# Low halves of the MLP's weights made by an accumulating DMA instead of a subtraction on VectorE

## The chip, the cores and the metric

The kernel runs on one core of one Trainium2 chip. The core has a matrix engine (TensorE, PE in the profile; PEld are its weight loads), a vector engine (VectorE, DVE), a scalar engine (ScalarE, ACT), a general engine (GpSimd, POOL) and a queue engine (SyncE, SP), each with its own program, and 16 DMA engines that move data between HBM and the on-chip SBUF. Matmul results go to PSUM. The metric is the device time of one execution in microseconds (us), the median of several runs.

## The reference

One layer of a streaming encoder on x of [1, 512, 1024] in float32: three token mixers side by side, their gated sum and an output projection, a cross-attention into 256 memory tokens, and then the gated MLP that this case is about:

```
def conv_ffn(h, w_up, conv_w, conv_b, w_down):
    u = causal_dwconv(h @ w_up, conv_w) + conv_b
    a, b = jnp.split(u, 2, axis=-1)
    return (jax.nn.silu(a) * b) @ w_down
...
        x = x + conv_ffn(rmsnorm(x, norm_ffn[l]), w_up[l], ffn_conv[l], ffn_conv_b[l], w_down[l])
```

`w_up` is [1024, 5632] and `w_down` [2816, 1024], both float32; the convolution is causal, of width 3.

## The kernel before

All activations lie with channels on the 128 partitions and the 512 tokens along the row. The weights come as a stream of 168 units of [128, 1024] float32 (512 KB), eight blocks of [128, 128] each. TensorE multiplies in a rounded 32-bit format (fp32r in the profile). To keep float32 accuracy, each weight unit and each activation tile is cut in two: a high part, which is the value rounded to fp32r, and a low part, which is the value less the high part. A product then takes three matmuls for each block: high by high, high weights by low activations, low weights by high activations.

A unit is handled by three lines. `load_unit` (L139 to L146) has SP load it from HBM into a `wraw` buffer. `split_unit` (L148 to L156) has ACT write the rounded copy into a `whi` buffer (L154) and DVE write the difference of `wraw` and `whi` into a `wlo` buffer (L155). `WB = (3, 2, 2)` gives the number of buffers: three for `wraw`, two each for `whi` and `wlo`. A buffer is filled anew when its last reader is done. `mm3` (L171 to L178) issues a unit's matmuls: for each of its eight blocks the two with the high weights (L175, L176), and then the eight with the low weights (L178), a *low run* below. So a unit costs 24 matmuls, 16 with `whi` and 8 with `wlo`.

The MLP is the last part. Its up projection (L879 to L893) goes over 22 pairs of output tiles, one unit each: 44 units, through `project` (L183). The result `up` is scaled by `r_f` (L885, the norm's factor, on DVE), put through the convolution (`uc`: one step on ACT, L887, and two on DVE, L889), and after each second unit through silu on ACT (L891) and a product on DVE (L892), which is split again into `hid` tiles (L162 on ACT, L163 on DVE). The norm's factor `r_f` is worked out at the start of the MLP from a matmul `xfps` (L871) through three steps on ACT (`rfa`, `rfb`: L216 to L218) and three on DVE. The down projection (L895 to L908) goes over 8 output tiles `dn`, each over 22 blocks, so that a unit can end in the middle of a tile: 22 units, through `split_unit` (L902). Its results are added to the residual (L907) and stored by SP (L908).

The order of the instructions on each engine isn't that of the code. A scheduler places them by its own simulated timeline, with the data dependencies and the buffers as limits; each engine then runs its own list in order, and an instruction that waits holds up all that stand behind it on its engine. POOL has no instruction in the MLP, and issues no DMA anywhere.

Of the kernel before, what the change touches and what calls it, by code (L numbers as in the profile page):

```python
# [36 lines left out]

# [1 line left out]
COLS = {}  # L39
# [15 lines left out]

# [1 line left out]
UNITS = {}  # L57
# [9 lines left out]
def build(nc, tc, ctx, x_t, mem_t, w, cols_d, const_d, unit_d, out_t, dbg=None):  # L67
# [13 lines left out]

    work = tiles_of("work", "n", 4)        # short-lived
    awork = tiles_of("work", "w", 8)
# [29 lines left out]
    def in_one_go(after, tiles, func):  # L113
        """func on tiles in place, behind the instruction `after`, with one load of its table"""
        with tc.issue_after(after.ins), tc.high_priority():
            for t in tiles:
                S.activation(t, t, func)
            exp_ln_tables()
# [16 lines left out]

# [1 line left out]
    units = {}  # L137
# [10 lines left out]
    def split_unit(u):  # L148
        """a unit of the weight stream as an exact sum of two float32r operands"""
        raw = units.pop(u) if u in units else load_unit(u)  # L150
        hi = wp.tile([P, 1024], F32R, tag="whi", name=f"whi{u}", bufs=WB[1])
        lo = wp.tile([P, 1024], F32R, tag="wlo", name=f"wlo{u}", bufs=WB[2])
        for s in [slice(0, T), slice(T, 2 * T)] if u == 0 else [slice(0, 2 * T)]:
            S.activation(hi[:, s], raw[:, s], AF.Copy)  # L154
            V.tensor_tensor(lo[:, s], raw[:, s], hi[:, s].bitcast(F32), ALU.subtract)  # L155
        return hi, lo  # L156

    def split(src, alloc, name):
        """src as hi + lo"""
        hi = alloc(name + "h", F32R)  # L160
        lo = alloc(name + "l", F32R)
        S.activation(hi, src, AF.Copy)  # L162
        V.tensor_tensor(lo, src, hi.bitcast(F32), ALU.subtract)  # L163
        return hi, lo
# [6 lines left out]
    def mm3(ps, unit, blocks, xs, first, last):  # L171
        """ps += the blocks of a unit times xs, without the product of the low parts"""
        hi, lo = unit
        for i, (b, (xh, xl)) in enumerate(zip(blocks, xs)):
            PE.matmul(ps, hi[:, b], xh, start=first and i == 0, stop=False)  # L175
            PE.matmul(ps, hi[:, b], xl, start=False, stop=False)  # L176
        for i, (b, (xh, _)) in enumerate(zip(blocks, xs)):
            PE.matmul(ps, lo[:, b], xh, start=False, stop=last and i == len(xs) - 1)  # L178

    def block(i, n=P):  # L180
        return slice(i * P, i * P + n)

    def project(u, xs, name, n=T):  # L183
        ps = dense_ps(name)
        mm3(ps[:, :n], split_unit(u), [block(k) for k in range(KC)], xs, True, True)
        return ps
# [16 lines left out]
    def project_heads(u, ys, name, n=4):  # L203
        """[512, 1024] weights, two output tiles in a unit"""
        for g in range(n):
            unit = split_unit(u + g)
            for q in range(2):
                ps = dense_ps(f"{name}{2 * g + q}")
                mm3(ps, unit, [block(4 * q + k) for k in range(4)], ys, True, True)
                yield 2 * g + q, ps  # L210

    def rsqrt(ps, name, scale, n=T, work=work):
        """-2 / sqrt(ps * scale + eps), with a Newton step"""
        a = work(name + "a", F32, n)
        b = work(name + "b", F32, n)
        S.activation(a, ps, AF.Ln, bias=eps, scale=scale)  # L216
        S.activation(a, a, AF.Exp, scale=-0.5)
        S.activation(b, a, AF.Square, scale=math.sqrt(scale))  # L218
        V.scalar_tensor_tensor(b, ps, EPS / scale, b, ALU.add, ALU.mult)
        V.scalar_tensor_tensor(a, b, -3.0, a, ALU.add, ALU.mult)  # L220
        return a

    def head_norm(src, name, scale, n=T, work=work, psum=misc_ps, light=False):
        """-2 / sqrt(sum of src^2 * scale + eps) on every partition"""
        sq = work(name + "s", F32, n)
# [47 lines left out]

# [1 line left out]
    hs = []  # L275
# [14 lines left out]

# [1 line left out]
    xs, acc = [], None  # L292
# [10 lines left out]
    V.tensor_scalar(r_x, rsqrt(ps, "rx", 1.0 / D), -0.5, None, ALU.mult)  # L303
# [1 line left out]
    gl = cp.tile([P, H, 4], F32, tag="gl", name="gl")  # L305
# [36 lines left out]
    def convolve(g, base):  # L342
        """silu(conv(projection)) of the tiles of q, k or v"""
        conv[g] = cs = [ptile(f"{g}{h}") for h in range(H)]
# [6 lines left out]

# [1 line left out]
    R = 96  # L353
# [7 lines left out]
    def scalars():  # L361
# [24 lines left out]
        V.tensor_tensor(rl[:R], rows[:R], rh[:R].bitcast(F32), ALU.subtract)  # L386
        # token on partition: [.., token block, row]
        ps = misc_ps("rcol")
# [3 lines left out]
        V.tensor_scalar(ngc, rc[:, :, 2], -1.0, None, ALU.mult)  # L392
        # beta, beta * exp(gc), exp(g_last - gc)
        S.activation(beta, rc[:, :, 1], AF.Exp)
# [3 lines left out]
    def select(ps, kind, h, stop=True):  # L398
        """a row of the scalars on every partition"""
        sel = sp.tile([P, P], F32R, tag="sel", name=f"sel_{kind}{h}")  # L400
# [19 lines left out]
    def prep_head(h):  # L420
# [5 lines left out]
        q, k = cq, ck  # L426
        # the decay, [j, i] by chunks, 0 for j > i
        pt = gdn_ps(f"pt{h}")
# [11 lines left out]
        S.activation(tail[:, :, h], tail[:, :, h], AF.Exp)  # L440
        # A^T without its factors beta_i, and attn^T
        pk = gdn_ps(f"pk{h}")
# [13 lines left out]
        V.tensor_tensor(att, pq, et, ALU.mult)  # L456
        # token-major keys and values
        pkt = gdn_ps(f"pkt{h}")
# [11 lines left out]

    # the inverses of the 32 x 32 diagonal blocks of I + A by elimination, a block's
    # even or odd columns on a partition
    inverse = []
# [29 lines left out]
    def expand(dst, src, h):  # L503
        """the 32 x 32 blocks of a head on the diagonals of its chunks"""
        G.tensor_tensor(dst.rearrange("p (t m c) -> p t m c", t=4, m=4),
                        src[:, 4 * h:4 * h + 4, None, :].to_broadcast([P, 4, 4, 32]),
                        cst("blk")[:, None, :, None].to_broadcast([P, 4, 4, 32]), ALU.mult)
# [10 lines left out]
    def invert(h):  # L518
        """(I + A)^-T of the chunks from that of the blocks on their diagonals: with D these and
        M = A D^-1 without these blocks, M^4 = 0 and (I + A)^-1 = D^-1 (I - M + M^2 - M^3)"""  # L520
        xcomp, ycomp = inverse
# [46 lines left out]
    def qkv_head(u, h, name, norm, alloc):  # L568
        """q^T, k^T and [key, dv] by key blocks"""
        out = alloc(h)  # L570
# [19 lines left out]
    def packed(name, kinds):  # L590
        """[P, 128], .. [P, 512] of each kind, the halves of a kind's tile shared"""
        out, half = [], None
# [9 lines left out]

# [1 line left out]
    ya = []  # L604
# [40 lines left out]

# [1 line left out]
    mixed = []  # L647
# [20 lines left out]

# [1 line left out]
    tri_r = cp.tile([P, 2, P], F32R, tag="tri_r", name="tri_r")  # L670
# [42 lines left out]

# [1 line left out]
    sz, yb = [], []  # L715
# [62 lines left out]

# [1 line left out]
    xs_mem = split_mem(mem_sb, "mem", ztile)  # L780
# [7 lines left out]

# [1 line left out]
    acc = None  # L790
# [11 lines left out]

# [1 line left out]
    def memory_key(h):  # L804
# [69 lines left out]

# [1 line left out]
    cross.close()  # L876
    open_pool("hidden", ctx)
    hid = []
    for m in range(NF):  # L879
        ab = []  # L880
        for z in range(2):
            j = m + NF * z
            ps = project(UNITS["up"] + 2 * m + z, xf, f"up{j}")
            u = awork(f"u{j}")
# [11 lines left out]
    for m in range(KC):  # L896
        ps = dense_ps(f"dn{m}")
        k = 0
        while k < NF:
            c = m * NF + k  # L900
            if c % 8 == 0:
                unit = split_unit(UNITS["down"] + c // 8)  # L902
            n = min(8 - c % 8, NF - k)
# [23 lines left out]
def unit_columns():  # L927
    """[P, 32, 16]: the even (on even partitions) or odd columns of the unit matrix"""
    i = np.arange(P)
# [3 lines left out]
def layout(inputs):  # L933
# [3 lines left out]
    def tiles(a, n):  # L937
        """[K, M] -> [units, P, 1024] streaming (output tile, k chunk) blocks of [P, 128]"""
        k, m = a.shape
# [5 lines left out]
    def tokens(a):  # L945
        """[1024, 512] -> [4, P, 1024] streaming k chunks"""
        return a.reshape(4, 2, P, 512).transpose(0, 2, 1, 3).reshape(4, P, 1024)

    def by_head(a):
        """[q | k | v] weights as q, k, v of a head after the other"""  # L950
        return tiles(a, 12).reshape(3, H, P, 1024).transpose(1, 0, 2, 3).reshape(12, P, 1024)
# [75 lines left out]
```

## Time and profile before

| | us |
|---|---|
| median of 3 runs | 1073.2 |
| lowest and highest run | 1072.76 and 1074.09 |
| span of the profiled execution, first to last instruction | 1072.4 |

The page gives for the profiled execution's own time its span, 1072.4 us. In it, the MLP's first matmul starts at 699.54 us and its last low run at 1066.78, so that the MLP with its end takes about a third of the time. The page's 40 slices show the four compute engines and the DMA engines; each digit is the busy share of a slice of 26.8 us in tenths:

```profile
PE   6999999999999999999999998999999999999998
DVE  5987566886454443454577667667776667742221
ACT  6689677856263646574546557544444444431110
POOL 0000100101010000000000000000000000000000
PEclk9999999999999999999999999999999999999999
DMA  5232212121211122122244233122222222233330
```

The MLP is the last 14 of the 40. The queue table shows what the DMA engines carry (packets, MB, share of the 16 engines' span); q1 is SP's:

```profile
q1 hardware_dynamic: 27648, 95.26, 27.1%
HBM read 93.41 MB, written 2.10 MB: 89 GB/s over the span
```

### The profile page before, as it was taken

The numbers are of one execution on the slowest core, as the hardware profiler recorded it, in microseconds if no ns is written. First come the engines' busy times: TensorE is split into PE (matmuls) and PEld (weight loads), VectorE is DVE, ScalarE is ACT, GpSimd is POOL, SyncE is SP. The second block draws the span as 40 slices with busy tenths as digits, with TensorE's granted clock in tenths as the row PEclk, the third lists the DMA queues.
The fourth block names the chain that finished last, engine by engine and source line by source line (L and its number), as shares of the span: only waits on it lengthen the run. The fifth ranks groups of instructions, "written<-read, shape, count | busy, mean of one in ns | idle before, by whom it ended". The sixth has DMA issues, their size and how long they took to land.

```text
span 1072.4 us, 12705 instructions
## 1 busy us (share of the span) xinstructions
PE 1055.4 (98%) x4868; PEld 858.3 (80%) x4868; DVE 638.3 (60%) x1002; ACT 556.3 (52%) x894; POOL 31.6 (3%) x81
## 2 busy tenths in 40 slices
PE   6999999999999999999999998999999999999998
PEld 4887888778888888888888886778888888888886
DVE  5987566886454443454577667667776667742221
ACT  6689677856263646574546557544444444431110
POOL 0000100101010000000000000000000000000000
PEclk9999999999999999999999999999999999999999
DMA  5232212121211122122244233122222222233330
GB/s 209 79 98 98 79 61 77 61 88 59 80 59 60 59 64 74 60 65 97 94 147 168 90 107 99 41 97 99 90 90 95 98 99 92 91 103 108 118 117 20
DMA packets 27853, 96.33 MB, mean 90 GB/s; under 512 B 3088, under 2 KB 3344, under 8 KB 27536
## 3 DMA queue, kind: packets, MB, share of 16 engines
q1 hardware_dynamic: 27648, 95.26, 27.1%
q8 instruction: 38, 0.62, 0.2%
q10 hardware_dynamic: 144, 0.26, 0.1%
q14 instruction: 23, 0.19, 0.1%
HBM read 93.41 MB, written 2.10 MB: 89 GB/s over the span
## 4 chain that ended last, share of the span: by engine, by line
PE 96%; DVE 1%; ACT 1%; DMA 1%; issue 0%; SPq 0%; DVEq 0%; ACTq 0%
PE up L176 8%; PE up L178 8%; PE up L175 8%; PE g L176 4%; PE g L175 4%; PE g L178 4%; PE dn L178 4%; PE dn L176 4%; PE dn L175 4%; PE wo L176 1%; PE s L175 1%; PE f L178 1%; PE f L175 1%; PE s L176 1%; PE wo L178 1%; PE wo L175 1%
## 5 line engine op out<-in xcount | busy, mean ns | idle before, releaser
L154 ACT ACTIVATE whi<-wraw 128x1024 fp32r<-128x1024 f32 (+1 forms) x168 | 177.1, 1054 | 286.0 <-PE up L176 86.1
L155 DVE TENSOR_TENSOR wlo<-wraw,whi 128x1024 fp32r<-128x1024 f32 (+1 forms) x168 | 204.7, 1219 | 144.2 <-PE dn L178 49.2
L176 PE MATMUL up<-xfl,whi 128*128 128x512 f32 x352 | 139.3, 396 | 0.0
L175 PE MATMUL up<-xfh,whi 128*128 128x512 f32 x352 | 138.7, 394 | 0.0
L178 PE MATMUL up<-xfh,wlo 128*128 128x512 f32 x352 | 88.9, 395 | 0.0
L178 PEld LDWEIGHTS up<-xfh,wlo 128*128 128x128 f32 x352 | 66.3, 188 | 15.7 <-issue 0.2
L176 PEld LDWEIGHTS up<-xfl,whi 128*128 128x128 f32 x352 | 66.3, 188 | 15.7 <-issue 0.2
L175 PEld LDWEIGHTS up<-xfh,whi 128*128 128x128 f32 x352 | 66.3, 188 | 15.5
L175 PE MATMUL g<-hh,whi 128*128 128x512 f32 x192 | 76.9, 401 | 0.0
L176 PE MATMUL g<-hl,whi 128*128 128x512 f32 x192 | 76.8, 400 | 0.0
L889 DVE SCALAR_TENSOR_TENSOR uc<-u,cols,uc 128x511 f32<-128x511 f32 (+1 forms) x88 | 65.3, 747 | 1.4
L887 ACT ACTIVATE uc<-u,cols 128x512 f32<-128x512 f32 x44 | 35.8, 816 | 45.2 <-DVE u L885 45.0
L885 DVE TENSOR_TENSOR u<-up,r_f 128x512 f32<-128x512 f32 x44 | 30.2, 688 | 40.4 <-PE up L178 40.4
L178 PE MATMUL g<-hh,wlo 128*128 128x512 f32 x192 | 52.3, 402 | 0.0
L178 PEld LDWEIGHTS g<-hh,wlo 128*128 128x128 f32 x192 | 35.9, 188 | 8.3 <-issue 0.2
L176 PEld LDWEIGHTS g<-hl,whi 128*128 128x128 f32 x192 | 36.2, 188 | 7.8 <-issue 0.2
L175 PEld LDWEIGHTS g<-hh,whi 128*128 128x128 f32 x192 | 36.2, 188 | 7.7
L175 PE MATMUL f<-hh,whi 128*128 128x512 f32 x64 | 26.0, 406 | 0.0
L175 PE MATMUL s<-hh,whi 128*128 128x512 f32 x64 | 25.7, 402 | 0.0
L176 PE MATMUL s<-hl,whi 128*128 128x512 f32 x64 | 25.5, 398 | 0.0
L176 PE MATMUL wo<-msl,whi 128*128 128x512 f32 x64 | 25.3, 396 | 0.0
L176 PE MATMUL f<-hl,whi 128*128 128x512 f32 x64 | 25.3, 395 | 0.0
(968 smaller groups left out, 2288.1 us busy)
## 6 DMA issues: line engine op xcount, KB each, us to landing
wraw<-w SPq DMA_DIRECT2D x166, 512.0 KB, 3.3
x<-x_t SPq DMA_DIRECT2D x8, 256.0 KB, 7.2
xr<-x_t SPq DMA_DIRECT2D x2, 1024.0 KB, 6.2
out<-out SPq DMA_DIRECT2D x8, 256.0 KB, 2.0
mem_sb<-mem_t SPq DMA_DIRECT2D x4, 256.0 KB, 6.5
wraw<-w SPq DMA_DIRECT2D x2, 256.0 KB, 4.7
inv<-unit ACTq DMA_DIRECT2D x1, 256.0 KB, 3.9
const<-const SPq DMA_DIRECT2D x1, 194.0 KB, 6.4
```

The source lines that it names most:

```text
L154: S.activation(hi[:, s], raw[:, s], AF.Copy)
L155: V.tensor_tensor(lo[:, s], raw[:, s], hi[:, s].bitcast(F32), ALU.subtract)
L175: PE.matmul(ps, hi[:, b], xh, start=first and i == 0, stop=False)
L176: PE.matmul(ps, hi[:, b], xl, start=False, stop=False)
L178: PE.matmul(ps, lo[:, b], xh, start=False, stop=last and i == len(xs) - 1)
L885: V.tensor_tensor(u, ps, r_f, ALU.mult)
L887: S.activation(c, u, AF.Identity, bias=col("ffn_conv_b", j), scale=col("ffn_conv", 3 * j + 2))
L889: V.scalar_tensor_tensor(c[:, s:], u[:, :T - s], col("ffn_conv", 3 * j + 2 - s), c[:, s:], ALU.mult, ALU.add)
```

## The change

In the MLP's 66 units, and in no others, the low part is made in another way. ACT writes the negative of the rounded unit into the `wlo` buffer; then a DMA that POOL issues reads the unit from HBM a second time and adds it to what lies in the buffer. What is left is the unit less its rounded value, which is what DVE's subtraction gave. ACT still writes `whi` from `wraw`, and SP still loads `wraw`. DVE has no part in it any more.

```diff
+    def split_unit_adding(u):
+
+        raw = load_unit(u)
+        lo = wp.tile([P, 1024], F32R, tag="wlo", name=f"wlo{u}", bufs=WB[2])
+        hi = wp.tile([P, 1024], F32R, tag="whi", name=f"whi{u}", bufs=WB[1])
+        S.activation(lo, raw, AF.Copy, scale=-1.0)
+        G.dma_start(lo, w[u], accum_op=ALU.add)
+        S.activation(hi, raw, AF.Copy)
+        return hi, lo
...
-    def project(u, xs, name, n=T):
+    def project(u, xs, name, n=T, split=split_unit):
         ps = dense_ps(name)
-        mm3(ps[:, :n], split_unit(u), [block(k) for k in range(KC)], xs, True, True)
+        mm3(ps[:, :n], split(u), [block(k) for k in range(KC)], xs, True, True)
         return ps
...
-            ps = project(UNITS["up"] + 2 * m + z, xf, f"up{j}")
+            ps = project(UNITS["up"] + 2 * m + z, xf, f"up{j}", split=split_unit_adding)
...
-                unit = split_unit(UNITS["down"] + c // 8)
+                unit = split_unit_adding(UNITS["down"] + c // 8)
```

The rest of the diff takes comments away. In the changed kernel the new lines are L163 (the negative), L164 (POOL's DMA) and L165 (the rounding), and what stood behind L157 has a number higher by 10.

The scheduler orders the engines' lists anew. In the rows below, a row is a line of the kernel, the operation, and the tile it writes and those it reads, with what it waits for (DMAHW is a load of SP, DMASW a DMA of POOL); the numbers behind tile names only tell tiles apart. First ACT, in the middle of the up phase. Before, two units' worth:

```order
L154 ACTIVATE whi_6860<-wraw_6858 128x1024 [waits DMAHW7_49,PE_49]
L162 ACTIVATE hid10h<-uc_6767 128x512 [waits DVE_49]
L887 ACTIVATE uc_6810<-u_6808,cols 128x512 [waits DVE_49]
L154 ACTIVATE whi_6897<-wraw_6895 128x1024 [waits DMAHW0_49,PE_49,Activation_49]
L891 ACTIVATE uc_6810<-uc_6810 128x512 [waits DVE_49,Activation_49]
L887 ACTIVATE uc_6847<-u_6845,cols 128x512 [waits DVE_49]
```

And ACT at the same place now:

```order
L165 ACTIVATE whi_6923<-wraw_6920 128x1024 [waits DMAHW0_49,PE_49]
L172 ACTIVATE hid10h<-uc_6789 128x512 [waits DVE_49]
L163 ACTIVATE wlo_6884<-wraw_6882 128x1024 [waits DMASW6_49,PE_49]
L897 ACTIVATE uc_6833<-u_6831,cols 128x512 [waits DVE_49]
L165 ACTIVATE whi_6967<-wraw_6964 128x1024 [waits DMAHW1_49,PE_49,Activation_49]
L901 ACTIVATE uc_6833<-uc_6833 128x512 [waits DVE_49,Activation_49]
L163 ACTIVATE wlo_6922<-wraw_6920 128x1024 [waits DMASW7_49,PE_49]
L897 ACTIVATE uc_6871<-u_6869,cols 128x512 [waits DVE_49]
```

Each unit has one more instruction, L163, ahead of the convolution's step; it waits for PE, whose low run of two units earlier reads the same buffer. The rounding of the next unit now comes ahead of a unit's negative.

Then TensorE near the start of the up phase, around the low run of the MLP's unit 3 (its tiles end in 6014 and 6018 before, in 6017 and 6020 now). Before:

```order
L175 MATMUL up_6014<-xfh_5815,whi_6017 128x512
L176 MATMUL up_6014<-xfl_5816,whi_6017 128x512
L178 MATMUL up_6014<-xfh_5725,wlo_6018 128x512 x4
L178 MATMUL up_6014<-xfh_5815,wlo_6018 128x512 x4
L175 MATMUL up_6057<-xfh_5725,whi_6060 128x512 [waits DVE_49,Activation_49]
```

TensorE at the same place now:

```order
L186 MATMUL up_6061<-xfl_5726,whi_6065 128x512
L185 MATMUL up_6061<-xfh_5725,whi_6065 128x512
L188 MATMUL up_6017<-xfh_5725,wlo_6020 128x512 [waits DMASW3_49]
L188 MATMUL up_6017<-xfh_5725,wlo_6020 128x512 x3
L188 MATMUL up_6017<-xfh_5815,wlo_6020 128x512 x4
L186 MATMUL up_6061<-xfl_5726,whi_6065 128x512
```

A unit's low run has moved behind the first matmuls with the high weights of the unit after it: seven of them here, 16 further on. It waits for POOL's DMA where it waited for DVE. Unit 2 isn't moved so: its low run still follows on its own 16 matmuls with `whi`.

Last POOL, which had no row in the MLP, from its last row of the attention on:

```order
L711 AFFINE_SELECT s_3366<-s_3366 128x128 [waits Activation_49,Pool_49]
L164 DMA wlo_5900<-w 128x1024 [waits DVE_49,Activation_49]
L164 DMA wlo_5938<-w 128x1024 [waits DVE_49,Activation_49]
L164 DMA wlo_5982<-w 128x1024 [waits DMASW0_49,Activation_49]
L164 DMA wlo_6020<-w 128x1024 [waits DMASW1_49,Activation_49]
```

It goes on like this for 66 rows: each waits for ACT's negative and for the DMA that filled the same buffer two units earlier.

## The prediction, made before the changed kernel was run

> **What bounds the kernel now.** I read the page's busy shares first, then the stages the change touches (the MLP, from 699 us to the end), then the chain of work that ended last.
>
> ```profile
> PE 1055.4 (98%) x4868; PEld 858.3 (80%) x4868; DVE 638.3 (60%) x1002; ACT 556.3 (52%) x894; POOL 31.6 (3%) x81
> PE 96%; DVE 1%; ACT 1%; DMA 1%; issue 0%; SPq 0%; DVEq 0%; ACTq 0%
> 750.00:800.00 50.00, 50.00 (x217) 40.55 (x216) 34.89 (x45) 21.32 (x27) 0.00 (x0) 1.00 0.28 93
> 1000.00:1050.00 50.00, 50.00 (x217) 40.54 (x216) 13.01 (x12) 9.43 (x9) 0.00 (x0) 1.00 0.30 101
> ```
>
> The first row gives TensorE 98% of the span, the second 96% of the chain that ended last. The last two are 50 us of the up projections and 50 us of the down projections: after the length come the busy times of PE, its weight loads, DVE, ACT and POOL, the granted clock (1.00), the DMA engines' share and GB/s. TensorE is busy for all 50 of 50 us in both, at full clock. DVE has 15 and 37 us free, ACT 29 and 41. So in the stages changed, nothing that DVE is spared can reach the end: there is no TensorE wait to remove.
>
> How fast TensorE goes through a unit is read from the chain (start, length, what):
>
> ```profile
> 754.46 1.87 PE up L178 x8
> 793.50 1.87 PE up L178 x8
> ```
>
> Both are runs of eight low-half matmuls; 39.04 us apart is seven units, so a unit of 24 matmuls takes 5.58 us and a matmul 0.2324 us. That is my clock for everything below.
>
> **The change part by part.** 66 of the 168 units are split in another way. Taken away from DVE and added to ACT:
>
> ```profile
> L155 DVE TENSOR_TENSOR wlo<-wraw,whi 128x1024 fp32r<-128x1024 f32 x65 | 79.2, 1218 | 69.9 <-PE dn L178 49.2 <-ACT whi L154 15.1 <-ACT rfa L217 5.6
> L154 ACT ACTIVATE whi<-wraw 128x1024 fp32r<-128x1024 f32 x65 | 68.9, 1060 | 176.3 <-PE up L176 86.1 <-PE dn L176 83.9 <-issue 6.3
> ```
>
> These are the groups from 699 us on (count, busy us, mean ns, idle before). DVE loses 66 subtractions of 1.22 us, 80 us in all; no one waits for DVE on the path, so this is worth nothing. ACT gains 66 negatives of the same shape as its rounding, 1.06 us each, 70 us in all. In the up phase its 21.3 us of 50 become 30.8 (nine units a 50 us), in the down phase 9.4 become 19. It stays off the path by load. A second load on HBM of 512 KB for each unit comes to 35 MB.
>
> What decides is a latency. The low half of a unit was: one DVE instruction. It is now: ACT's negative, a hand-over to POOL, POOL's DMA, landing. Behind the waiting negative on ACT stand the convolution's `uc` and the next rounding; behind the waiting matmul on TensorE stands everything. POOL has nothing else to do in this stage, so nothing stands behind its wait but the next unit's DMA. SP's loads now wait for ACT instead of DVE to free `wraw`, at about the same time, and are needed two units later.
>
> I call L the time from POOL's issue to landing, and ask how much L can be. `wlo` has two buffers, so the negative of a unit starts when the low run of the unit two before has ended, and the low run of the unit itself is due two units (11.16 us) less one low run (1.86) later. From these 9.30 us go the negative (1.06) and three hand-overs; I allow 0.08 each (estimate; ACT to DVE took 0.03 here, 873.20 to 873.23):
>
> ```profile
> 872.58 0.62 ACT L162 ACTIVATE hid14h<-uc 128x512 fp32r<-128x512 f32 x1
> 873.23 0.69 DVE L163 TENSOR_TENSOR hid14l<-uc,hid14h 128x512 fp32r<-128x512 f32 x1 [1.33 <-ACT hid14h L162]
> ```
>
> That leaves **8.0 us in the steady state**. The new order of TensorE, which puts up to 16 high-half matmuls of the next unit ahead of a low run, delays the start and the due time alike and doesn't alter the 8.0. Above it each further microsecond costs half a microsecond a unit, 33 us over 66 units.
>
> Two places have less. Unit 2, where the MLP begins (before):
>
> ```profile
> 707.60 2.02 PE L178 MATMUL up<-xfh,wlo 128*128 128x512 f32 x8
> 708.15 1.05 ACT L154 ACTIVATE whi<-wraw 128x1024 fp32r<-128x1024 f32 x1
> 709.10 0.62 ACT L217 ACTIVATE rfa<-rfa 128x512 f32<-128x512 f32 x1
> 711.54 0.39 PE L175 MATMUL up<-xfh,whi 128*128 128x512 f32 x1
> ```
>
> Unit 2's negative comes behind the `rfa` step on ACT, so it runs from 709.8 to 710.8 and POOL issues at 710.9; its low run follows directly on its 16 high matmuls, at 711.54 + 16 x 0.2324 = 715.3. Less a hand-over, **4.3 us** are left. The second is the down phase's unit 1, where between the low run of the last up unit and its own only 4 + 8 + 16 = 28 matmuls stand: 6.51 - 1.06 - 0.24 = **5.2 us**. Half a dozen more, 36 or 37 matmuls apart, leave 7.1 to 7.3. Walking ACT, DVE and TensorE through their rows in the new order with these durations gives, in us of TensorE waiting: 0 at L = 4.3, 0.7 at 5.0, 2.1 at 5.8, 3.3 at 6.4, 4.3 at 6.9, 10.4 at 7.9, 38 at 9.0, 50 at 9.4, 102 at 11.
>
> Now L, which no row shows, since no accumulating DMA and none from POOL is in the trace. The nearest rows:
>
> ```profile
> wraw<-w SPq DMA_DIRECT2D x166, 512.0 KB, 3.3
> xr<-x_t SPq DMA_DIRECT2D x2, 1024.0 KB, 6.2
> inv<-unit ACTq DMA_DIRECT2D x1, 256.0 KB, 3.9
> 10.00:15.00 5.00, 4.70 (x9) 2.70 (x10) 4.90 (x7) 5.00 (x9) 0.00 (x0) 1.00 1.05 405
> ```
>
> The first three give KB and median us to landing, the last a stretch in which the engines moved 405 GB/s. At that rate 512 KB take 1.3 us, so 2.0 of the 3.3 us are fixed. The lower end is a DMA that costs what a plain load costs, 3.3 us: no loss. A gain is excluded by the 50 of 50 us. For the value, an addition has to fetch the weights and the old `wlo`, twice 1.3 us; SP's load of a later unit is set free by the same negative and goes beside it, 1.3 more; 2.0 + 2.6 + 1.3 = 5.9, near the 6.2 of the `xr` pair, which also moves more than one load's bytes at once. For POOL making the transfer in software I add 0.5 (estimate, from SP's 0.33 an issue): **L = 6.4**. For the upper end I let the addition go at a quarter of the plain rate: 2.0 + 5.2 + 1.3 + 0.5 = 9.0; up to 9.4 stays in the range. The engines' total also allows it: 0.28 of 50 us is 1.6 us a unit now, with twice that again 4.7 of 5.58.
>
> **The sum.** 2.1 us at unit 2 and 1.2 at the down phase's unit 1: 3.3 us on a span of 1072.4. The page gives no time for its execution but this span; the median of the timed runs, 1073.2, is 0.8 above it, which I keep. 1073.2 + 3.3 = **1076.5 us**.
>
> **The rivals.**
> - *The landing is quick enough, not slower.* Place: the low run of unit 2. If the addition costs little beyond a plain load, L under 5.8, the loss is under 2.1 us and can't be told from no change (a measurement of this kernel tells about 0.2%, 2.1 us); at 4.3 and below it is 1073.2 exactly. For it: 3.3 us of the plain load, free engines for 70% of the time. Against: the load beside it, the second fetch. Beside it stand two rules that no run here shows: the Trainium skill's page "DMA: Bandwidth & Descriptors", section "Anatomy of one DMA — SWDGE (gpsimd) path", gives a DMA from GpSimd 2.0 us and its bytes at 436 GB/s, and its page "Collectives: The Full Stack", section "The bandwidth ceiling: the fold count and why AG ≠ RS ≠ AR", says that an addition in the DMA engine costs a second source read and nothing for the arithmetic. An estimate from both pages, 2.0 + 2 x 1.2 = 4.4 us with nothing beside it, would make the loss 0.1 us.
> - *The landing is late in every unit.* Above 8.0, the wait repeats 66 times: at 9.0 it is 1073.2 + 38 = 1111, at 11 it is 1175. For it: everything in L that is unknown is on this side. Against: it needs the addition at below a third of the plain rate.
> - *POOL is kept from writing its transfer by DVE.* DVE's longest stretch in a unit is two `uc` steps:
>
> ```profile
> 875.57 1.53 DVE L889 SCALAR_TENSOR_TENSOR uc<-u,cols,uc 128x511 f32<-128x511 f32 x2
> ```
>
> If POOL had to wait it out, L would be 6.4 + 1.5 = 7.9 and the loss 10.4: 1083.6. Against: only 35 of 50 us are DVE's, 24 once the subtraction is gone. The Trainium skill's page "SBUF — State Buffer", section "Who interferes with whom", has the rule: GpSimd is locked out of its SBUF ports while DVE is in a two-port mode, and a DVE instruction with two SBUF inputs blocks GpSimd's reads. No run here shows it.
> - *It doesn't do what it is said to.* TensorE would have to gain; the freed DVE time would have to shorten the start of the MLP. That is under 2 us at most.
>
> **How the numbers follow.** Landing between 5.8 and 7.3 us, the forecast: 0.36. Quick enough, within 0.2%: 0.28. DVE in POOL's way: 0.10. Late in every unit: 0.24. A gain above 0.2%: 0.02. So slower 0.70, same 0.28, faster 0.02. The range goes from L = 4.6 (0.3 us, 1073.5) to L = 9.4 (1073.2 + 50, rounded up to 1125), and leaves out about a tenth at either end.
>
> **What would show it.** Right: POOL's DMAs land 5.8 to 7.3 us after issue; TensorE waits once near 715 us and once near 950 us, each 1 to 3 us, for a DMA into `wlo`, and stays at 50 of 50 us between. ACT about 31 of 50 us in the up phase. Wrong to the good: landing below 5. Wrong to the bad: the 50 us windows of the up phase show PE under 48 and low-run matmuls waiting for `wlo` some 60 times; then L is above 8 and the size of the addition's cost was the error. A wrong mechanism: TensorE waiting for `whi` or ACT, or SP's loads landing much later than 3.3 to 4.8 us.

## The result: 1.8% slower, and the profile after

| | before | after |
|---|---|---|
| median of the timed runs, us | 1073.4 (4 runs) | 1092.7 (4 runs) |
| lowest to highest, us | 1072.8 to 1074.1 | 1090.9 to 1095.8 |
| ratio | | 1.0182 [1.0165, 1.0200] |
| the profiled execution: span, us | 1072.4 | 1089.1 (timed at 1090.9) |
| matmuls, 690 to 730 us | 172 | 147 |
| matmuls, 730 to 950 us | 949 | 925 |
| matmuls, 950 to 1060 us | 475 | 449 |

The changed kernel is 19.3 us slower; 1076.5 was forecast, with a range of 1073.5 to 1125. The page of after, its busy shares, the chain that ended last and the DMA issues:

```profile
PE 1063.2 (98%) x4868; PEld 857.4 (79%) x4868; DVE 566.6 (52%) x936; ACT 622.9 (57%) x960; POOL 88.6 (8%) x147
PE 83%; DMA 11%; ACT 2%; issue 2%; DVE 1%; SPq 0%; POOLq 0%; DVEq 0%; ACTq 0%
wraw<-w SPq DMA_DIRECT2D x166, 512.0 KB, 3.4
wlo<-w POOLq DMA_DIRECT2D x66, 512.0 KB, 7.7
```

The first row alone would mislead: PE is busy 98% as before. A matmul's record lasts 0.39 us and the next one starts 0.23 us after it, so a short delay leaves no idle time in the records, and matmuls that run at a lower clock count as busy too. The chain is plainer: 11% of it is now DMA, where 96% was PE. The last row is the new one: a unit's addition takes 7.7 us from issue to landing.

Where the time went is read from windows that follow the stages: the start of the MLP, the up phase, the down phase. Before:

```profile
690.00:730.00 40.00, 40.00 (x172) 32.12 (x171) 30.43 (x43) 21.81 (x30) 0.00 (x0) 1.00 0.29 93
730.00:950.00 220.00, 220.00 (x949) 178.34 (x948) 153.80 (x199) 93.83 (x119) 0.00 (x0) 1.00 0.29 95
950.00:1060.00 110.00, 110.00 (x475) 89.20 (x474) 29.86 (x28) 21.43 (x21) 0.00 (x0) 1.00 0.31 100
```

And after, in the same columns (length, busy time of PE, its weight loads, DVE, ACT and POOL, granted clock, DMA share, GB/s):

```profile
690.00:730.00 40.00, 36.07 (x147) 28.50 (x146) 19.89 (x31) 23.17 (x31) 4.50 (x5) 0.96 0.63 145
730.00:950.00 220.00, 218.04 (x925) 172.67 (x924) 108.30 (x153) 130.26 (x155) 32.75 (x38) 1.00 0.84 181
950.00:1060.00 110.00, 106.37 (x449) 83.31 (x448) 12.72 (x18) 42.92 (x43) 17.29 (x20) 1.00 0.91 199
```

Count the matmuls, not the busy time: 25, 24 and 26 are missing, and at 0.2324 us each that is 5.8, 5.6 and 6.0 us, 17.4 of a span that grew by 16.7. So in this execution a third of the loss belongs to each stage. The waits from 690 us on (engine and line, what it waited for, us in all, times, longest) say for what:

```profile
PE up L188 <- DMA wlo<-w: 6.0, 7, 3.9
PE dn L188 <- DMA wlo<-w: 3.2, 4, 2.0
PEld up L188 <- DMA wlo<-w: 13.0, 18, 4.4
PEld dn L188 <- DMA wlo<-w: 7.3, 11, 2.4
```

Every large wait is for POOL's DMA into `wlo`. PE and its weight loads wait for the same landing at the same low run, and a weight load's wait lies partly under running matmuls, so the four rows do not add up to the loss. They have at most 29 units between them (18 and 11), out of 66: this is not a wait in every unit.

What costs 4 us at once is at the start, unit 2 (start, length, what, in brackets the idle time before it):

```profile
708.90 1.06 ACT L163 ACTIVATE wlo<-wraw 128x1024 fp32r<-128x1024 f32 x1
710.25 0.86 POOL L164 DMA_DIRECT2D wlo<-w  x1 [8.97 <-ACT wlo L163]
718.59 2.92 PE L188 MATMUL up<-xfh,wlo 128*128 128x512 f32 x8 [3.93 <-DMA wlo<-w]
```

And a unit in the steady state:

```profile
782.32 1.06 ACT L163 ACTIVATE wlo<-wraw 128x1024 fp32r<-128x1024 f32 x1 [0.29 <-PE up L188]
783.41 0.33 SPq L145 DMA_DIRECT2D wraw<-w  x1
783.68 0.86 POOL L164 DMA_DIRECT2D wlo<-w  x1 [4.72 <-ACT wlo L163]
```

Two things are to be seen. POOL starts 0.30 us after ACT's negative has ended (783.38), where the prediction allowed 0.08: of its 8.0 us of allowance 7.8 are left, and the landings' median is 7.7. And the same negative frees `wraw`, so SP's load of a later unit is issued 0.27 us ahead of the addition: two transfers of 512 KB start together. What that is worth is the subject of the experiments.

### The profile page after: what moved, and what is told of

Its sections match the earlier page's. It is cut to its first block, busy times and chain, and to the rows that moved or that the text cites. A ratio compares the mean times of both kernels' runs of the same rounds, so it can differ in the third digit from the quotient of the medians.

```text
span 1089.1 us, 12904 instructions
## 1 busy us (share of the span) xinstructions
PE 1063.2 (98%) x4868; PEld 857.4 (79%) x4868; DVE 566.6 (52%) x936; ACT 622.9 (57%) x960; POOL 88.6 (8%) x147
## 4 chain that ended last, share of the span: by engine, by line
PE 83%; DMA 11%; ACT 2%; issue 2%; DVE 1%; SPq 0%; POOLq 0%; DVEq 0%; ACTq 0%
DMA wlo<-w 10%; PE up L188 6%; PE up L185 5%; PE up L186 5%; PE g L185 4%; PE g L186 4%; PE g L188 4%; PE dn L188 3%; PE dn L186 2%; PE dn L185 2%; PE wo L186 1%; PE f L188 1%; PE s L185 1%; PE f L185 1%; PE s L186 1%
## 5 line engine op out<-in xcount | busy, mean ns | idle before, releaser
L154 ACT ACTIVATE whi<-wraw 128x1024 fp32r<-128x1024 f32 (+1 forms) x102 | 107.1, 1050 | 107.3 <-PE g L186 34.1
L155 DVE TENSOR_TENSOR wlo<-wraw,whi 128x1024 fp32r<-128x1024 f32 (+1 forms) x102 | 124.3, 1219 | 74.5 <-PE g L188 36.6
L165 ACT ACTIVATE whi<-wraw 128x1024 fp32r<-128x1024 f32 x66 | 69.9, 1059 | 116.0 <-PE up L186 57.6
L164 POOL DMA_DIRECT2D wlo<-w x66 | 57.1, 866 | 561.6 <-ACT wlo L163 561.6
L163 ACT ACTIVATE wlo<-wraw 128x1024 fp32r<-128x1024 f32 x66 | 70.0, 1060 | 54.3 <-PE up L188 29.1
L188 PE MATMUL up<-xfh,wlo 128*128 128x512 f32 x352 | 91.4, 402 | 6.2 <-DMA wlo<-w 6.0
L917 DVE TENSOR_TENSOR out<-dn,xr 128x512 f32<-128x512 f32 x8 | 5.5, 692 | 112.3 <-PE dn L188 112.3
```

The source lines that it names most:

```text
L163: S.activation(lo, raw, AF.Copy, scale=-1.0)
L164: G.dma_start(lo, w[u], accum_op=ALU.add)
L165: S.activation(hi, raw, AF.Copy)
L917: V.tensor_tensor(o, ps, x3[m], ALU.add)
```

## The experiments

The theory after the result (A): the addition lands late since SP's load goes beside it; the landing sits on the allowance of two low tiles, and the start costs some 5 us by itself. The rivals: the DMA engines are short of time, whatever the tiles allow (B); the addition takes that long by itself, load or not (C). In all experiments the ratio is to the kernel before, run on the same chip.

### A third low tile

```
-        lo = wp.tile([P, 1024], F32R, tag="wlo", name=f"wlo{u}", bufs=WB[2])
+        if (u - UNITS["up"]) % 3 == 2:
+            lo = pool["mlo"].tile([P, 1024], F32R, tag="mlo", name=f"wlo{u}", bufs=1)
+        else:
+            lo = wp.tile([P, 1024], F32R, tag="wlo", name=f"wlo{u}", bufs=WB[2])
...
+    open_pool("mlo", ctx)
```

> Every third unit of the MLP puts its low half in one more buffer, so three buffers take turns instead of two; everything else of the change stays. Theory A (two buffers leave about 7.8 us from a negative's DMA issue to its due time, and the landing takes 7.7): the allowance grows by one unit, 5.58 us, to about 13, so the waits of the low runs for wlo go from 29 us to under 3, and the time is 1073.5 to 1076 us. Rival B (the DMA engines, busy 0.83 to 0.91 of the MLP, are what bounds it): a buffer more changes nothing in the rate, the time stays at 1088 or more and the landing grows.

Measured: 1072.9 us, ratio 0.9991 [0.9982, 1.0000]. All waits of TensorE are gone, at a DMA share that is no smaller than in the changed kernel:

```profile
730.00:950.00 220.00, 220.00 (x951) 178.74 (x950) 111.68 (x158) 134.79 (x159) 33.64 (x39) 1.00 0.84 189
wlo<-w POOLq DMA_DIRECT2D x66, 512.0 KB, 5.4
```

A share of 0.84 and PE at 220 of 220 us: B falls, the engines are not short. But the landing fell too, to 5.4 us, which was not the plan: with the third tile the scheduler puts the negative ahead of the rounding, so the rounding frees `wraw` and SP's load leads the addition by 2.07 us (median) instead of 0.27. The run changes the allowance and the lead at once, and does not tell which of them did it.

### No load beside the addition

```
-        raw = load_unit(u)
+        raw = units["mlp"] = units.get("mlp") or load_unit(u)
```

> The MLP's 66 units all use the one raw tile that the first loads, so SP's 512 KB loads are gone from the MLP (65 of them; the products use other weights than the reference), while the negatives and the accumulating DMAs are all there. Theory A (the load that the same negative sets free costs the addition its share of the DMA engines): the landing falls from 7.7 to 5.0 to 5.6 us, as the last two in the changed kernel, 5.4 and 5.3, which have no load beside them; what is left is about 1 us at unit 2, so 1074 to 1077 us. Rival C (the addition itself, with POOL making it in software, is what is slow): the landing stays at 7 us or more and the time at 1088 or more.

All MLP units take their rounded half from the first unit's raw tile, and the low half is the unit less that, so that it is no longer small; the two halves still add up to the unit, so the weights are the reference's, and not others as the expectation says. 65 loads are left out. Measured: 1074.5 us, ratio 1.0009 [1.0000, 1.0018]. The landing:

```profile
wlo<-w POOLq DMA_DIRECT2D x66, 512.0 KB, 5.4
```

So the addition alone takes 5.4 us, and the load beside it costs 2.3 more. C falls. The landing is what this run can show; its time is no clean comparison, since the scheduler also set the low runs of the down phase more evenly (37 to 40 matmuls apart instead of 28 to 43), and in the up phase 945 matmuls start where the kernel before has 949, with no wait to explain it. In the changed kernel itself the last two additions, which have no load beside them, landed after 5.4 and 5.3 us.

### The same DMA without the addition

```
-        G.dma_start(lo, w[u], accum_op=ALU.add)
+        G.dma_start(lo, w[u])
```

> POOL's DMA only copies the unit over the negative, without adding (the low half is then the whole unit). Same instructions and same order. Theory A: the engines' time of one goes from 2.97 us to about that of SP's load, 1.6 to 1.7, so the landing falls by about 1.3 us to 6.2 to 6.6, below the 7.8 that the buffers leave; the time is 1075 to 1080 us. Rival C' (POOL's software path, not the addition, makes it slow): the landing stays above 7.2 us and the time above 1084.

Measured: 1074.5 us, ratio 1.0007 [0.9998, 1.0016], with the load still 0.27 us ahead. Here and in the changed kernel (the second pair of rows), the group of POOL's issues and the queue's packets, MB and share of 16 engines:

```profile
L164 POOL DMA_DIRECT2D wlo<-w x66 | 35.0, 531 | 566.0 <-ACT wlo L163 552.3
q0 software_dynamic: 9504, 34.61, 9.0%
wlo<-w POOLq DMA_DIRECT2D x66, 512.0 KB, 4.6
```

```profile
L164 POOL DMA_DIRECT2D wlo<-w x66 | 57.1, 866 | 561.6 <-ACT wlo L163 561.6
q0 software_dynamic: 9504, 34.61, 18.0%
```

9.0% of 1071.6 us over 66 units is 1.46 us of all engines for a unit; 18.0% of 1089.1 is 2.97. The addition doubles the engines' time at the same bytes, and POOL's own issue grows from 0.53 to 0.87 us. The landing of a plain DMA is 4.6 us beside a load, under the 6.2 to 6.6 that was expected (the time is 0.5 us under its range too), and 3.5 to 3.6 for the last three, which have no load beside them. TensorE's matmuls stand in the same order here as in the changed kernel, so this run differs by the addition alone. So a load that starts together with it costs a plain DMA 1.0 us and an addition 2.3, and 3.1 of the 7.7 us are the addition's.

### The first units by subtraction

```
-            ps = project(UNITS["up"] + 2 * m + z, xf, f"up{j}", split=split_unit_adding)
+            ps = project(UNITS["up"] + 2 * m + z, xf, f"up{j}", split=split_unit if m < 2 else split_unit_adding)
```

> The MLP's first four units keep DVE's subtraction, the other 62 add. Theory A: the start's wait at unit 2 (3.9 us) and the slow matmuls behind it (about 2 us at 0.42 us each instead of 0.23) go, 5 to 6 us, and the rest stays: 1086 to 1088 us. Rival D (the wait only moves to the first unit that adds): 1091 us or more, with one long wait at unit 4 or 5.

Measured: 1087.7 us, ratio 1.0130 [1.0114, 1.0145], 5.0 us less than the changed kernel. The start is whole again, the rest is not:

```profile
690.00:730.00 40.00, 40.00 (x172) 32.10 (x171) 27.51 (x40) 22.89 (x31) 1.88 (x2) 1.00 0.44 117
730.00:950.00 220.00, 216.19 (x918) 171.49 (x917) 107.08 (x150) 128.67 (x153) 32.75 (x38) 1.00 0.85 180
```

172 matmuls are those of the kernel before. The start term is real and is about 5 us. The rest is no fixed amount: with the same lead, the same landing (7.8 us) and, but for its first units, the same spacing of the low runs, 918 matmuls stand in the up phase and 436 in the down phase, where the changed kernel's profiled execution has 925 and 449.

### The negative from the rounded unit

ACT rounds first and takes the negative from `whi`; the rounding then frees `wraw`. Two low tiles, as in the change.

```
-        S.activation(lo, raw, AF.Copy, scale=-1.0)
-        G.dma_start(lo, w[u], accum_op=ALU.add)
         S.activation(hi, raw, AF.Copy)
+        S.activation(lo, hi.bitcast(F32), AF.Copy, scale=-1.0)
+        G.dma_start(lo, w[u], accum_op=ALU.add)
```

> ACT rounds first and writes the negative from the rounded unit, so that the rounding frees the raw tile and SP's next load is issued about 1.9 us ahead of POOL's addition instead of 0.27 us ahead of it; still two low tiles, and the same allowance. Theory (the landing of 7.7 us came from both transfers starting together): landing 5.3 to 6.0 us, the waits for the low halves nearly gone but for unit 2, 1074 to 1077 us. Rival (addition and load share the 16 engines whatever their phase, and only the tile count mattered in the run with a third tile): landing stays at 7 us or more and the time at 1088 us or more.

Measured: 1077.8 us, ratio 1.0045 [1.0030, 1.0060], 0.8 over the upper end that was expected.

```profile
690.00:730.00 40.00, 37.54 (x154) 29.71 (x153) 20.59 (x32) 24.45 (x32) 5.37 (x6) 0.96 0.66 158
730.00:950.00 220.00, 220.00 (x948) 178.37 (x948) 112.16 (x159) 134.49 (x158) 33.72 (x39) 1.00 0.83 188
wlo<-w POOLq DMA_DIRECT2D x66, 512.0 KB, 5.5
```

The loads lead by 2.9 us (median; 2.9 or 3.3 in most of the up phase, 2.2 in most of the down phase), more than the 1.9 that was expected; the additions land after 5.5, and the up phase has its 948 matmuls again, with the same 40 matmuls between the end of one low run and the start of the next but one. The loads are all there, only earlier. Of the waits one is left, unit 2's (2.5 us), and it explains why the time is over the expectation: 18 matmuls are missing there, 4.2 us. For the down phase (475 matmuls, all there) this run is no clean comparison, since the scheduler also set its low runs more evenly, 36 to 40 matmuls apart instead of 28 to 43.

### POOL delayed on purpose: three lengths

One more pass on POOL (a multiplication by 1) stands between the negative and the addition. It does nothing but make POOL's addition later and so give the load, which follows the negative, a lead. First over all 1024 columns:

```
         S.activation(lo, raw, AF.Copy, scale=-1.0)
+        G.tensor_scalar(lo, lo.bitcast(F32), 1.0, None, ALU.mult)
         G.dma_start(lo, w[u], accum_op=ALU.add)
```

> The changed kernel with one more pass on POOL over the low tile (a multiplication by 1, about 2.1 us by POOL's 1.04 to 1.09 us for 512 columns) between ACT's negative and POOL's addition. The load is still issued behind the negative, so it now starts about 2 us ahead of the addition. Theory (start together is what costs): landing falls to about 5.4 us, the chain from negative to landing is 2.1 + 5.4 = 7.5 us against 7.7, and the time stays near the changed kernel's, 1085 to 1100 us. Rival (landing is 7.7 us whatever the phase): the chain grows by 2.2 us in every unit, over the allowance of about 7.8, and the time goes to some 1150 to 1165 us.

Measured: 1186.7 us, ratio 1.1048 [1.1026, 1.1069]. The time is past even the rival's, and yet the median landing is the theory's. The rows show that, one pair of units, and the landings of that pair's two additions:

```profile
wlo<-w POOLq DMA_DIRECT2D x66, 512.0 KB, 5.5
740.99 5.51 POOL L164 TENSOR_SCALAR wlo<-wlo 128x1024 fp32r<-128x1024 f32 x2 [8.24 <-ACT wlo L163]
746.46 1.81 POOL L165 DMA_DIRECT2D wlo<-w  x2
751.83 2.13 PE L189 MATMUL up<-xfh,wlo 128*128 128x512 f32 x8 [2.31 <-DMA wlo<-w]
DMA to landing us min/median/max: 5.3/6.3/7.4
```

The size of the pass was wrong: 2.77 us where 2.1 was expected, and the scheduler ran the passes in pairs, both ahead of both DMAs. The first of a pair is thus used 10.9 us after its negative has ended (740.90 to 751.83), and TensorE waits 2.3 us for it here and 2 to 3 us for nearly every pair of the up phase. The median of 5.5 hides two kinds of landing: the first of a pair lands after 5.3 us, as the theory has it, and the second, issued 0.9 us later, after 7.4, although its load leads by more. So another addition that starts just ahead costs about as much as a load does, and the lead over the load is not the whole account. The time could not tell the two theories apart, as the expectation had it. So the pass was made shorter, over 64 and over 256 columns, where it stays one pass, one DMA:

```
+        G.tensor_scalar(lo[:, :64], lo[:, :64].bitcast(F32), 1.0, None, ALU.mult)
```

> The changed kernel with one short pass on POOL ahead of the addition, over the first 64 of the low tile's 1024 columns (a multiplication by 1, about 0.2 to 0.3 us). SP's load then leads the addition by about 0.6 us instead of 0.27. Theory (the lead decides the landing): the landing falls between 7.7 us (lead 0.27) and 5.5 us (lead 2.2), about 7.3; chain unchanged, time 1085 to 1095 us. Rival (the lead decides nothing, landing 7.7): the chain is 0.3 us longer in every unit and the time 1098 to 1106 us.

> The same with a pass over 256 of the 1024 columns (about 0.7 to 0.9 us); the load leads by about 1.1 us. Theory: landing about 6.5 us, chain 0.8 + 6.5 = 7.3 us, time 1078 to 1092 us, no slower than the changed kernel although POOL does more. Rival (landing 7.7 whatever the lead): chain 8.5 us, 0.7 us over the allowance, time 1110 to 1125 us.

Measured: 1091.6 us, ratio 1.0177 [1.0160, 1.0194], with 64 columns; 1085.8 us, ratio 1.0124 [1.0102, 1.0145], with 256. The passes took 0.36 and 0.85 us. The additions land after 7.1 us with 64 columns and 6.0 with 256. Put together, with the lead as the median time from SP's issue to POOL's:

| run | lead, us | landing, us | matmuls, 730 to 950 us | matmuls, 950 to 1060 us | time, us |
|---|---|---|---|---|---|
| the change | 0.27 | 7.7 | 925 | 449 | 1092.7 |
| pass over 64 columns | 0.73 | 7.1 | 929 | 440 | 1091.6 |
| pass over 256 columns | 1.21 | 6.0 | 937 | 440 | 1085.8 |
| third tile | 2.07 | 5.4 | 951 | 476 | 1072.9 |
| negative from `whi` | 2.9 | 5.5 | 948 | 475 | 1077.8 |
| no load | none | 5.4 | 945 | 473 | 1074.5 |

The landing falls with the lead from 7.7 to the 5.4 that it takes alone; 2.1 us of lead are enough. The kernel with 256 columns does more work and takes 6.8 us less. Its chain has one step more and is yet shorter: 0.10 + 0.85 + 0.30 + 6.0 = 7.3 us from the end of the negative to the landing, against 0.30 + 7.7 = 8.0.

The time follows the landing less plainly. Most of the 6.8 us are the start's: with 256 columns unit 2's low run was set behind more matmuls (41 instead of 25 after unit 0's), which takes away the wait there, and 169 matmuls stand between 690 and 730 us instead of 147, worth 5.1 us. The up phase gains 12 matmuls, 2.8 us, and the down phase loses 9, 2.1 us. In the up phase's steady part the same 40 matmuls stand between the low runs in all the rows. There the matmuls missing from the 949 go from 24 to 20 and 12 with the two passes, and to 1 with the negative from `whi`. With the lead still at 0.27 us the run with the first units subtracted misses 31, so 24 and 20 are no difference; 12 and 1 are. In the down phase that run misses 39 of 475 and the two passes 35 each: there no gain from the lead is seen in the time, though the landing fell there too (7.3 and 6.0 us).

### Both cures together

The negative from `whi`, and the first four units by subtraction.

> The negative from the rounded unit, and the first four MLP units by DVE's subtraction as before the change. If the late landing and the start are all of the loss: no wait for a low half of over 1 us left, 1073 to 1075 us, the same as the kernel before. If something else of the change costs (traffic in HBM, ACT's 70 us more): 1078 us or more with TensorE busy 50 of 50 us in the MLP all the same, or with waits for other tiles.

Measured: 1073.8 us, ratio 1.0003 [0.9994, 1.0013], the same as before the change.

```profile
690.00:730.00 40.00, 40.00 (x172) 32.08 (x172) 27.39 (x40) 23.55 (x32) 2.17 (x3) 1.00 0.46 132
730.00:950.00 220.00, 220.00 (x948) 178.40 (x947) 114.04 (x158) 131.91 (x159) 34.28 (x40) 1.00 0.82 188
```

Nothing else of the change costs anything that could be measured here: not ACT's 62 further instructions, not the second read of the weights. Alone, the first cure took back 14.9 us (1092.7 to 1077.8) and the second 5.0 (to 1087.7); together 18.9.

## Why the prediction came out as it did

**What bounds the kernel: right.** TensorE was the limit, what DVE was spared was worth nothing (the page has it at 566.6 us after 638.3), and no run was clearly faster than before; the nearest is the third tile's, 0.9991 [0.9982, 1.0000]. ACT's 70 us stayed off the path: in the run with the third tile, where TensorE waited for nothing, ACT is busy for 134.8 of 220 us in the row shown there.

**The mechanism and the sign: right; the size: not.** TensorE waits for POOL's DMA into `wlo` and for nothing else new, at unit 2 and at the first units of the down phase, as named. But two waits were forecast, with nothing between them, and some 29 units wait. The loss was put at 3.3 us and is 19.3, so the time lies in the range because the range went up to L = 9.4, not because the sum was near. The landing, 7.7 us, is above the forecast's 5.8 to 7.3 and below the 8.0 from which a wait in every unit was expected. Even at that landing the walk would have been short: it gave 10.4 us at L = 7.9. One sign that was named for a wrong mechanism does show: between 750 and 940 us SP's loads land after 5.2 us, where 3.3 to 4.8 was allowed and the kernel before has 3.3. The page's 3.4 is a median over the whole program and hides it. It cost next to nothing: in the MLP ACT waited for a load once, 2.0 us. But it shows that the load and the addition hold each other up.

**The landing, L = 6.4: too low by 1.3 us.** Its terms were 2.0 fixed + 2.6 for two fetches + 0.5 for POOL = 5.1 for an addition alone; it took 5.4. The doubled engine time was right (2.97 against 1.46 us for a unit). The Trainium skill's page "Collectives: The Full Stack", section "The bandwidth ceiling: the fold count and why AG ≠ RS ≠ AR", has that rule, a second source read and nothing for the arithmetic, and these shares agree with it. The 4.4 us that the prediction worked out from two pages for an addition alone were 1.0 too few. **The term that failed is SP's load beside it**: 1.3 us were added, its bytes' time; it costs 2.3 when both start together and nothing that can be seen when the load is 2.1 us ahead. The prediction had seen that both are freed by the same negative, and did not ask what the two starts do to each other.

**The allowance of 8.0 us: 0.2 too high,** by the hand-over from ACT to POOL. That alone would be nothing. But with 7.7 against 7.8 about half of the units are late, by a little each, and the steady state that was to cost nothing lost 5.6 us. A walk with one L for all units could not show this: the landings go from 5.3 to 9.8 us, and a late unit costs while an early one gives nothing back.

**Unit 2, 2.1 us: measured 5.8.** The place was right. Its own landing took 8.3 us (issue at 710.25, use at 718.59), so TensorE waited 3.9 us, near the 8.3 less 4.3 that the prediction's own allowance gives. Most of the other 1.9 us is the clock, which the prediction did not have:

```profile
718.50:723.00 4.50, 4.41 (x12) 3.47 (x13) 1.45 (x3) 1.45 (x2) 0.10 (x1) 0.63 0.36 73
```

After the wait the granted clock is 0.63 over 4.5 us, which takes 0.37 x 4.5 = 1.7 us; 12 matmuls stand there where the kernel before has 21.

**The down phase, 1.2 us: measured 6.0.** It was mis-sized by the same two steps, the landing and the spread of it; 11 weight loads wait there instead of one.

**The slope, 33 us for each us above the allowance: not tested.** The walk gave 102 us at L = 11, and the kernel with the full pass, with each pair's first low half 10.9 us after its negative, lost 113. But there only one unit of a pair is as late as that, and some 25 us are the clock's (0.979 over 1186.3 us), which the walk did not have; that the two numbers are near is luck.

**The rivals.** The quick landing would have needed less than 5.8 us; without a load beside it, it is so, with 5.4 us and no measurable loss. The late landing in every unit is what the full pass made; the change stayed at its edge. POOL kept by DVE is not what happened: the landing takes as long where DVE is nearly idle. The first row is of the up phase (750 to 800 us), the second of the down phase (1000 to 1050), where DVE is busy for 2.08 of 50 us:

```profile
wlo<-w POOLq DMA_DIRECT2D x8, 512.0 KB, 7.8
wlo<-w POOLq DMA_DIRECT2D x9, 512.0 KB, 7.7
1000.00:1050.00 50.00, 49.59 (x212) 39.31 (x211) 2.08 (x3) 18.48 (x18) 7.79 (x9) 1.00 0.91 202
```

The rule that was weighed for it, of the Trainium skill's page "SBUF — State Buffer", section "Who interferes with whom", thus does not show in this trace.

**Why the lead matters** can be read from the DMA engines' packets, by queue: q0 has POOL's additions, q1 SP's loads. The rows give packets, MB and share of the 16 engines for the 2 us from 1.5 to 3.5 us after an addition's issue. The first two are the changed kernel's (issue at 783.68), the last is the third tile's (issue at 783.82), where no packet of a load falls into the stretch:

```profile
q1 hardware_dynamic: 118, 0.43, 66.1%
q0 software_dynamic: 23, 0.07, 27.8%
```

```profile
q0 software_dynamic: 75, 0.31, 94.1%
```

Over the units between 760 and 940 us the medians are 18 packets of additions beside 99 of loads in the changed kernel, 47 beside 56 with 64 columns, 58 beside 12 with 256, and 70 beside none with the third tile or the negative from `whi`. So the addition's packets come late where the load's fall into their time, and a lead takes the load's out of it. **What stays open** is by what rule the engines choose between the two: a plain DMA of POOL's has 106 packets beside the same 99. Nor was a load tried that starts behind the addition.

## What to carry to other kernels

When a cheap instruction is replaced by a chain through a DMA, compare the chain's latency with what the buffers allow, and treat a landing within a few tenths of the allowance as late: only the late half of its spread counts. Ask which other transfer the same event sets free; here 2 us between two starts decided on 2 us of landing, and the cure was the order of two ACT instructions. And look at the first use of the new chain apart: there is no head start there.

## What the runs showed that was not expected

A single short wait of TensorE can cost 1.7 us more than itself. In the kernel with the negative from `whi` the wait is only 2.5 us, and the clock still falls:

```profile
717.02 3.27 PE L188 MATMUL up<-xfh,wlo 128*128 128x512 f32 x8 [2.46 <-DMA wlo<-w]
717.00:721.00 4.00, 3.98 (x11) 3.12 (x12) 0.67 (x2) 0.69 (x2) 0.00 (x0) 0.58 0.88 242
```

11 matmuls stand in these 4 us where the kernel before has 19. Yet the changed kernel's longest wait in the down phase, 2.0 us, left the clock at 1.00, and so did a longer one, 2.7 us, in the run with the first units subtracted (the last row, with a clock of 1.00 from 958 to 964 us):

```profile
963.47 0.50 PE L188 MATMUL dn<-hid0h,wlo 128*128 128x512 f32 x1 [2.00 <-DMA wlo<-w]
963.00:967.00 4.00, 3.53 (x15) 2.91 (x16) 1.57 (x3) 1.36 (x2) 0.01 (x1) 1.00 0.93 188
```

```profile
959.83 0.50 PE L188 MATMUL dn<-hid0h,wlo 128*128 128x512 f32 x1 [2.71 <-DMA wlo<-w]
```

The length of the gap alone does not decide. Ahead of the MLP, in code that no run changes, every trace has one gap of TensorE of 2.5 us (near 667 us); from 664 to 673 us the granted clock is then 0.81 in the kernel before and 1.00 in the run with the third tile. What decides between them, these runs do not show.

The Trainium skill's page "TensorE: Matmul & The Clock Gate", section "HAM oscillation — how this bites in real kernels", warns of gaps of TensorE over about 3.4 us. Here a gap of 2.5 us was enough in some executions, and one of 2.7 was not in another.

The other surprise is the price of an accumulating DMA beside a load that starts with it: 2.3 us, against 1.0 for a plain DMA in the same place.
